# Hybrid encoder block on one Trainium2 core: short convolutions as closures among the next group's steps, side-stream loads issued a pause ahead

## Chip, cores and metric

The kernel runs on one core of a Trainium2 chip. The metric is the device time of one launch in microseconds (us). Three runs of the kernel before took 2955.26 to 2956.12 us, median 2955.6.

## What is computed

One block of a hybrid encoder on 512 tokens of width 2048, in fp32. Cut to what this case touches (the merge gates, the output projection and the feed-forward part come after it and stay as they are):

```python
hn = rmsnorm(x, norm1_w[l])
proj = hn @ w_in[l]
conv_out = centred_depthwise_conv(proj[..., :SHORT_CONV_CH], conv_w[l], conv_b[l])   # 3 taps
hv, hx1, hx2 = split of conv_out[..., :3 * HW]            # hyena: 3 x 1024 columns
z = hx1 * long_conv(hv, kf[:, 0], hb[0])                  # FFT convolutions with learned filters
y_a = hx2 * long_conv(z, kf[:, 1], hb[1])
q, k = silu(conv_out[..., 3 * HW:])                       # mLSTM: 4 heads of 256
v, o, g = rest of proj                                    # values, output gate, 16 gate columns
h_fwd, h_bwd = mlstm_direction(q, k, v, g), and on the reversed sequence
y_b = sigmoid(o) * (h_fwd + h_bwd)
merge = rest[..., 2 * MW + N_MLSTM_GATES:]
x = x + (sigmoid(merge_a) * (y_a @ w_branch_a) + sigmoid(merge_b) * (y_b @ w_branch_b)) @ w_out
x = x + (silu(gate) * up) @ w_down                        # after a second rmsnorm
```

## The kernel before

Every fp32 product is made of three matrix products of halves (`mm3`, L70): an operand is split into a high half `h` (a rounding copy on ScalarE, ACT) and a low half `l` (operand minus high half, on VectorE, DVE). For the weights these are `wh` (L164) and `wl` (L165).

The first stage multiplies the normalised input by the columns of `w_in` for hyena, heads and output gate. It goes by column groups of 256: twelve for hyena (four quarters `q`, three kinds each), then per head one for q, one for k and one for v, and four for the output gate, in the order of `parts`. A group has 8 steps of two 128-row blocks of weights; a step ends with `yield`. Weights are loaded by SyncE (SP, L157) and split two units ahead of use (`Weights`, `AHEAD`).

When a hyena, q or k group ends, `conv_evac` takes its two PSUM tiles. For each it multiplies by the row scale out of PSUM into a padded tile `pp` (L332), makes the middle tap with the bias on ACT (L334), adds the first tap (L336) and the last (L339 for hyena, where the result is written in four residue classes, L342 for q and k, with a SiLU on ACT behind it), all on DVE. Then a store on GpSimd's queue (POOL) takes the result to DRAM: `d_hy` (L356), `d_q` and `d_k` (L366). A v group is copied out of PSUM by ACT and stored to `d_v` (L374).

Between the steps of the main stream, `drive` (L242) advances a side stream. Each main step gives it a credit of `RATIO` = 2.2 (at most twice that is kept), and each piece of side work that yields a number costs that number. The side stream takes turns between two generators. One makes the hyena filters (`filter_net`, then `spectra`) and, last, combinations of the input for the next stage (`combos_x`). The other makes the gates, `hyena(q)` for each quarter and `mlstm(h)` for each head as soon as their columns have been stored. A generator that yields `"pause"` is left alone until two main steps later.

`hyena(q)` loads four tiles of `d_hy` by POOL (L750), transposes them on TensorE (PE, L683) into split halves (L314, L315) and makes the convolutions. `mlstm(h)` loads q and k by SP (L804), splits them at once, makes the scores `S`, loads `d_v` (L823) and the gate rows (L837) by POOL, and stores its result `d_yb` by POOL (L893).

The next stage (`Winograd`, loads `r` and `wr` at L1006 by SP, splits at L997 and L998) begins when main and side stream are through. `combo_1` prepares parts of its operands from the last output-gate group on, in tiles of the same pool as the side stream's (`gt`); three of its calls come after the main stream.

Of the kernel before, what the change touches and what calls it, by code (L numbers as in the profile page):

```python
# [11 lines left out]
ALU = mybir.AluOpType  # L12
# [22 lines left out]
def hybrid_block_kernel(ctx, tc, x, norm1_w, w_in, conv_w, conv_b, filt_w1, filt_b1, filt_freq1,  # L35
# [187 lines left out]
    def group_v(w, c0, act, ahead=None):  # L223

        ps = [mm_ps() for _ in range(4)]
        units = w_units(w, 0, KB, c0)
        for u in range(0, KB, 2):
            h, l = next(units) if ahead is None else ahead.get(c0, u)
            for tb in range(4):
                ts = slice(tb * P, (tb + 1) * P)  # L230
                for k in range(2):
                    kb = u + k
                    aH, aL = act[kb]
                    mm3(ps[tb][:, 0:256], aH[:, ts], aL[:, ts], h[:, k, :], l[:, k, :],
                        kb == 0, kb == KB - 1)
            yield None
        yield ps

    tick = [0]
    PAUSE = 2  # L240

    def drive(main, side=None, rate=0):  # L242

        left = 0
        for _ in main:
            tick[0] += 1
            left = min(left + rate, 2 * rate)
            while side is not None and left > 0:
                r = next(side, "wait")
                if r == "wait":  # L250
                    break
                left -= r
# [71 lines left out]
        return t.rearrange("p (m c) -> p c m", c=4)  # L324


    def conv_evac(ps, blk, classed):
        n_tile[0] += 1
        pp = pr.tile([P, L + 2], F32, tag="pp", name=f"pp_{n_tile[0]}", bufs=2)
        nc.gpsimd.memset(pp[:, 0:1], 0.0)  # L330
        nc.gpsimd.memset(pp[:, L + 1:L + 2], 0.0)
        nc.vector.tensor_tensor(pp[:, 1:L + 1], ps, rbc, ALU.mult)  # L332
        y = st()
        nc.scalar.activation(y, pp[:, 1:L + 1], AF.Identity, bias=cb[:, blk:blk + 1],  # L334
                             scale=cw[:, 1, blk:blk + 1])
        nc.vector.scalar_tensor_tensor(y, pp[:, 0:L], cw[:, 0, blk:blk + 1], y, ALU.mult, ALU.add)  # L336
        y2 = st()
        if classed:
            nc.vector.scalar_tensor_tensor(classes(y2), natural(pp[:, 2:L + 2]), cw[:, 2, blk:blk + 1],  # L339
                                           natural(y), ALU.mult, ALU.add)  # L340
        else:
            nc.vector.scalar_tensor_tensor(y2, pp[:, 2:L + 2], cw[:, 2, blk:blk + 1], y, ALU.mult, ALU.add)  # L342
            nc.scalar.activation(y2, y2, AF.Silu)
        return y2

    def hyena_cols(q, after_first=()):
        for kind in range(3):
            if kind == 1:
                yield from after_first
            for r in first_group if q == 0 and kind == 0 else group_feat(  # L350
                    w_in, 0, KB, kind * HW + q * 256, X, ahead=ahead):
                if r is None:
                    yield
            for j in range(2):
                y = conv_evac(r[j], kind * 8 + 2 * q + j, True)
                nc.gpsimd.dma_start(d_hy[kind][2 * q + j], y)  # L356
        done.add(("hy", q))

    def head_cols(h):
        for base, blk0, dst in ((C_Q, 24, d_q), (C_K, 32, d_k)):  # L360
            for r in group_feat(w_in, 0, KB, base + h * 256, X, ahead=ahead):
                if r is None:
                    yield
            for j in range(2):
                y = conv_evac(r[j], blk0 + 2 * h + j, False)
                nc.gpsimd.dma_start(dst[2 * h + j], y)  # L366
        done.add(("qk", h))
# [139 lines left out]
    h2 = {}  # L507

    def filter_net():
        for m in range(4):  # L510
            t = gt()
            nc.gpsimd.dma_start(t, c_dft[m])
            hh = new(ph, f"dH{m}", dt=F32R)
            ll = new(ph, f"dL{m}", dt=F32R)
            nc.scalar.copy(hh, t)
            nc.vector.tensor_tensor(ll, t, hh.bitcast(F32), ALU.subtract)
            dft.append((hh, ll))
            yield 1
# [10 lines left out]
        nc.gpsimd.dma_start(zt[0:33], c_zt)  # L529

        def sin_layer(ps, b, fr):
# [83 lines left out]
    def spectrum(q, o):  # L615
# [11 lines left out]
            wt.append(t)  # L627
        row = gt()
        nc.sync.dma_start(row[0:1, 0:256], hyena_bias[0][o:o + 1, c0:c0 + 256])
        yield .1  # L630
        wpm = gt()
        nc.vector.tensor_tensor(wpm[:, 0:256], w3[:, 0:256], w3[:, 256:512], ALU.add)
        nc.vector.tensor_tensor(wpm[:, 256:512], w3[:, 0:256], w3[:, 256:512], ALU.subtract)
# [109 lines left out]
    def hyena(q):  # L743
# [9 lines left out]

        u = load(0)
        x1 = load(1)
        yield .1
        halves = []
        for ps in by_times(u):
            halves.append(gsplit(ps))
# [37 lines left out]
    def mlstm(h):  # L797
        yield from need("gates")
        yield from need(("qk", h))
        qs, ks = [], []  # L800
        for src, dst in ((d_q, qs), (d_k, ks)):
            for j in range(2):
                t = gt()
                nc.sync.dma_start(t, src[2 * h + j])  # L804
                dst.append(gsplit(t))
            yield .6
        yield "pause"
        S = []
        for sb in range(4):
# [7 lines left out]
            yield .3  # L817
        yield from need(("v", h))

        V = []  # L820
        for b in range(2):
            t = gt()
            nc.gpsimd.dma_start(t.rearrange("p (b c) -> p b c", b=2),  # L823
                                d_v[h][2 * b:2 * b + 2].rearrange("b p c -> p b c"))
            vh, vl = vt(), vt()
# [7 lines left out]
        yield .6  # L833

        def load_row(d):
            t = gt()
            nc.gpsimd.dma_start(t, d_rows[4 * d + h:4 * d + h + 1].to_broadcast([P, L]))  # L837
            return t

        def weights(d, sb, row):  # L840

# [13 lines left out]


        units = [(0, sb) for sb in (0, 1, 2, 3)] + [(1, sb) for sb in (3, 2, 1, 0)]
        row = load_row(0)
        yield "pause"
        acc_t = [gt(), gt()]  # L860
        nxt = weights(*units[0], row)
        row_b = load_row(1)
# [124 lines left out]
    class Winograd:  # L987
# [30 lines left out]
        def cols(self, c0, psf, loaded=None, after={}, late=None):  # L1018
# [52 lines left out]
            nc.vector.tensor_tensor(C[1][:, hi], p5, u2, ALU.add)  # L1071
            return C

    N_PLAIN = 4
    AHEAD = 2
    RATIO = 2.2
    side = turns(stream_b(), stream_a())

    parts = (("hy", 1), ("hd", 0), ("hy", 2), ("hy", 3), ("hd", 1), ("hd", 2), ("hd", 3))
# [5 lines left out]
    def w_in_cols():  # L1085
# [9 lines left out]
    drive(w_in_cols(), side, RATIO)  # L1095
    for i in range(5, 8):
        combo_1(i, gt)
    for _ in side:
        tick[0] += 1
    pr_cm.__exit__(None, None, None)  # L1100
# [386 lines left out]
```

## Time and profile before

| | us |
|---|---|
| median of 3 runs | 2955.6 |
| the profiled execution, its own time | 2956.98 |
| its span | 2955.0 |
| PE busy in the span | 2893.7 |
| DVE busy | 2112.5 |
| ACT busy | 1271.5 |
| POOL busy | 185.7 |
| PE busy between 50 and 890 us | 805.29 of 840 |

The span is the time from the first to the last instruction on the core. An engine's busy time counts its compute instructions; issuing a transfer isn't counted. A wait is listed with the instruction that waited and, behind an arrow, the one that released it. The rows name tiles without their numbers: `sd` and `mm` are PSUM tiles, `g` tiles of the side stream's pool, `st` and `pp` those of the short convolution. The granted clock is the share of full speed that the chip gave PE; 1.00 is 2.4 GHz, 0.50 is 1.2 GHz.

### The profile page before, as it was taken

The page shows a single profiled execution, that of the slowest core. Times are in us where ns is not written, and L with a number is a line of the kernel's source. Part 1 is how long each engine was busy: PE and PEld are TensorE (multiplying, and loading weights), DVE is VectorE, ACT ScalarE, POOL GpSimd, SP SyncE. Part 2 cuts the span into 40 slices and gives each one's busy share as a digit, 9 for nine tenths or more (in the row PEclk, how much of TensorE's full clock was granted, in tenths as well). Part 3 has the DMA queues.
Part 4 walks back from the last instruction along what each step waited for, and adds up shares of the span by engine and source line. Part 5 has one row for each costly group of instructions (what it writes and reads, how often), then busy time and mean ns, then how long its engine had stood idle before and what let it go on. Part 6 is the DMA issues. An engine that isn't in the chain of part 4 may idle for free.

```text
span 2955.0 us, 48209 instructions
## 1 busy us (share of the span) xinstructions
PE 2893.7 (98%) x18412; PEld 2614.7 (88%) x18412; DVE 2112.5 (71%) x3843; ACT 1271.5 (43%) x2258; POOL 185.7 (6%) x433
## 2 busy tenths in 40 slices
PE   8999999998989999999999999999999999999998
PEld 6788887887879999888899999999999998888886
DVE  6897868777659888645448888888888886233336
ACT  5334344334555454422445444444444444233224
POOL 1011011101110000100010000000000000000000
PEclk9999999999999999999999999999999999999999
DMA  5333343333344444843444333333333336334333
GB/s 175 108 118 115 114 125 125 107 100 122 124 139 134 131 126 129 271 132 104 136 125 136 121 116 115 121 123 115 119 118 115 120 103 213 101 115 128 121 114 128
DMA packets 285185, 377.01 MB, mean 128 GB/s; under 512 B 18013, under 2 KB 221147, under 8 KB 284953
## 3 DMA queue, kind: packets, MB, share of 16 engines
q1 hardware_dynamic: 261280, 301.19, 32.9%
q0 software_dynamic: 22272, 70.55, 7.0%
q8 instruction: 144, 2.36, 0.3%
q10 hardware_dynamic: 1401, 2.20, 0.2%
q14 instruction: 88, 0.72, 0.1%
HBM read 326.67 MB, written 47.20 MB: 127 GB/s over the span
## 4 chain that ended last, share of the span: by engine, by line
PE 89%; DVE 4%; DMA 3%; issue 2%; ACT 1%; POOL 0%; SPq 0%; ACTq 0%; DVEq 0%; POOLq 0%
PE mm L70 63%; PE sd L70 25%; DMA wr<-in_w_down_dram 1%; DMA g<-d_hy 1%; DVE wl L165 0%; DMA hl<-d_h 0%; PE sd L683 0%; DMA g<-d_k 0%; DVE st L339 0%; DMA xt<-in_x_dram 0%; DVE st L336 0%; DVE h L81 0%; PE sd L1246 0%; DVE s L1014 0%; DMA g<-d_q 0%
## 5 line engine op out<-in xcount | busy, mean ns | idle before, releaser
L165 DVE TENSOR_TENSOR wl<-wr,wh 128x512 fp32r<-128x512 f32 x512 | 350.3, 689 | 492.9 <-ACT wh L164 485.8
L164 ACT CAST wh<-wr 128x512 fp32r<-128x512 f32 x512 | 315.8, 620 | 763.9 <-PE mm L70 722.1
L70 PE MATMUL mm<-a,wh 128*128 128x512 f32 (+1 forms) x2136 | 626.5, 377 | 0.0
L70 PE MATMUL mm<-T,h 128*128 128x256 f32 x2592 | 471.1, 284 | 3.2 <-ACT h L997 3.2
L70 PE MATMUL sd<-T,h 128*128 128x256 f32 x2592 | 468.2, 283 | 0.0
L70 PEld LDWEIGHTS mm<-a,wh 128*128 128x128 f32 x2136 | 388.8, 190 | 69.8 <-issue 2.9
L70 PEld LDWEIGHTS mm<-T,h 128*128 128x128 f32 x2592 | 406.3, 193 | 3.7 <-ACT h L997 3.7
L70 PE MATMUL mm<-a,wl 128*128 128x512 f32 (+1 forms) x1068 | 400.3, 376 | 8.2 <-DVE wl L165 6.1
L70 PEld LDWEIGHTS sd<-T,h 128*128 128x128 f32 x2592 | 404.4, 192 | 0.0
L70 PE MATMUL mm<-wh,h 128*128 128x512 f32 x1280 | 394.8, 389 | 2.8 <-ACT h L80 2.5
L70 PE MATMUL mm<-T,l 128*128 128x256 f32 x1296 | 368.0, 284 | 0.5 <-DVE l L998 0.5
L997 ACT CAST h<-s 128x512 fp32r<-128x512 f32 x395 | 244.5, 620 | 286.3 <-PE sd L70 142.1
L70 PE MATMUL sd<-T,l 128*128 128x256 f32 x1296 | 366.9, 283 | 0.0
L70 PEld LDWEIGHTS mm<-wh,h 128*128 128x128 f32 x1280 | 240.1, 188 | 54.0 <-ACT h L80 3.2
L998 DVE TENSOR_TENSOR l<-s,h 128x512 fp32r<-128x512 f32 x395 | 270.2, 685 | 11.6 <-ACT h L997 9.0
L997 ACT CAST h<-r 128x512 fp32r<-128x512 f32 x285 | 176.6, 620 | 222.6 <-PE mm L70 111.6
L70 PE MATMUL mm<-wh,a 128*128 128x256 f32 (+1 forms) x1152 | 262.5, 321 | 0.0
L70 PEld LDWEIGHTS mm<-T,l 128*128 128x128 f32 x1296 | 249.7, 193 | 1.0 <-DVE l L998 1.0
L70 PE MATMUL mm<-wl,h 128*128 128x512 f32 x640 | 249.0, 389 | 0.3 <-DVE wl L165 0.3
L70 PEld LDWEIGHTS sd<-T,l 128*128 128x128 f32 x1296 | 248.9, 192 | 0.0
L70 PEld LDWEIGHTS mm<-a,wl 128*128 128x128 f32 x1068 | 202.4, 190 | 46.8 <-DVE wl L165 9.2
L998 DVE TENSOR_TENSOR l<-r,h 128x512 fp32r<-128x512 f32 x285 | 191.6, 686 | 48.0 <-ACT h L997 47.6
(369 smaller groups left out, 4367.6 us busy)
## 6 DMA issues: line engine op xcount, KB each, us to landing
r<-in_w_gate_up_dram SPq DMA_DIRECT2D x176, 512.0 KB, 3.9
wr<-in_w_in_dram SPq DMA_DIRECT2D x144, 512.0 KB, 3.8
wr<-in_w_down_dram SPq DMA_DIRECT2D x88, 512.0 KB, 3.8
r<-in_w_in_dram SPq DMA_DIRECT2D x32, 512.0 KB, 4.5
wr<-in_w_out_dram SPq DMA_DIRECT2D x32, 512.0 KB, 3.7
d_h<-xo POOLq DMA_DIRECT2D x44, 256.0 KB, 2.6
hl<-d_h SPq DMA_DIRECT2D x44, 256.0 KB, 3.4
d_g<-xo POOLq DMA_DIRECT2D x32, 256.0 KB, 4.3
```

The costliest lines, as they stand in the source:

```text
L70: nc.tensor.matmul(o, a, b, start=start, stop=stop)
L164: nc.scalar.copy(h, src)
L165: nc.vector.tensor_tensor(l, src, h.bitcast(F32), ALU.subtract)
L997: nc.scalar.copy(h, a)
L998: nc.vector.tensor_tensor(l, a, h.bitcast(F32), ALU.subtract)
```

## The change

`conv_evac` does only the two multiplications out of PSUM at the group's end. The rest of each convolution, with its store, becomes a closure in the list `later`. `drive` pops one closure at each following main step, ahead of the side stream, and takes 1.9 from the side stream's credit for it. The marks that let `hyena` and `mlstm` begin (`done`) are closures too, at no cost, behind the stores.

`RATIO` goes from 2.2 to 2.6. Loads of the side stream are issued together, with a pause before their first use: in `filter_net`, `spectrum`, `hyena` and `mlstm`. The q and k loads of `mlstm` go to POOL's queue in place of SP's. `group_v` starts with two of the four token blocks and makes up for the other two in its second step. `combo_1` uses the `pp` tiles instead of the pool `g`.

```diff
@@ group_v
+            for tb, v, (wh, wl) in ([(tb, u, (h, l)) for tb in (0, 1)] + ([(2, 0, first), (3, 0, first)] if u == 2 else [])
+                                    + ([(2, u, (h, l)), (3, u, (h, l))] if u else [])):
...
@@ drive
             left = min(left + rate, 2 * rate)
+            if later:
+                cost, work = later.pop(0)
+                work()
+                left -= cost
             while side is not None and left > 0:
@@ conv_evac
         nc.vector.tensor_tensor(pp[:, 1:L + 1], ps, rbc, ALU.mult)
-        y = st()
...
+        def rest():
+            y = st()
+            nc.scalar.activation(y, pp[:, 1:L + 1], AF.Identity, bias=cb[:, blk:blk + 1],
+                                 scale=cw[:, 1, blk:blk + 1])
+            nc.vector.scalar_tensor_tensor(y, pp[:, 0:L], cw[:, 0, blk:blk + 1], y, ALU.mult, ALU.add)
...
+            store(y2)
+
+        later.append((1.9, rest))
+
+    def store_to(dst):
+        return lambda t: nc.gpsimd.dma_start(dst, t)
@@ hyena_cols
-                y = conv_evac(r[j], kind * 8 + 2 * q + j, True)
-                nc.gpsimd.dma_start(d_hy[kind][2 * q + j], y)
-        done.add(("hy", q))
+                conv_evac(r[j], kind * 8 + 2 * q + j, True, store_to(d_hy[kind][2 * q + j]))
+        later.append((0, lambda: done.add(("hy", q))))
@@ hyena
         x1 = load(1)
-        yield .1
+        yield "pause"
@@ mlstm
-        for src, dst in ((d_q, qs), (d_k, ks)):
+        raw = []
+        for src in (d_q, d_k):
             for j in range(2):
                 t = gt()
-                nc.sync.dma_start(t, src[2 * h + j])
-                dst.append(gsplit(t))
-            yield .6
+                nc.gpsimd.dma_start(t, src[2 * h + j])
+                raw.append(t)
+        yield "pause"
+        for dst in (qs, ks):
+            for j in range(2):
+                dst.append(gsplit(raw.pop(0)))
+                yield .7
...
@@ before the end of the stage
+    def padded():
+        n_tile[0] += 1
+        return pr.tile([P, L + 2], F32, tag="pp", name=f"pp_{n_tile[0]}", bufs=2)[:, 0:L]
...
-    RATIO = 2.2
+    RATIO = 2.6
...
-                    combo_1(n - 3, gt)
+                    combo_1(n - 3, padded)
```

The change moves instructions on most engines of the first stage; from the first products of the next stage on, the order is as before. Three places follow.

DVE where the q group of head 2 ends. Before, with the convolution's L336 (first tap) and L342 (last tap) of both tiles, among pieces of a hyena convolution (L709 to L718), up to the next `wl`:

```order
L336 SCALAR_TENSOR_TENSOR st_6223<-pp_6219,cols_86,st_6223 128x512
L709 TENSOR_TENSOR g_6214<-g_6185,g_5315 128x512
L342 SCALAR_TENSOR_TENSOR st_6226<-pp_6219,cols_86,st_6223 128x512
L710 TENSOR_TENSOR g_6185<-g_6186,g_5314 128x512
L336 SCALAR_TENSOR_TENSOR st_6234<-pp_6230,cols_86,st_6234 128x512
L711 TENSOR_TENSOR g_6214<-g_6214,g_6185 128x512
L342 SCALAR_TENSOR_TENSOR st_6237<-pp_6230,cols_86,st_6234 128x512
L714 TENSOR_TENSOR g_6215<-g_6213 128x256
L715 TENSOR_TENSOR g_6215<-g_6214 128x256
L717 TENSOR_TENSOR g_6185<-g_6213 128x256
L718 TENSOR_TENSOR g_6185<-g_6214 128x256
L165 TENSOR_TENSOR wl_6269<-wr_6243,wh_6268 128x512
```

Twenty-eight DVE instructions stand there between one `wl` and the next. The same convolution on DVE in the change (L344 is the multiplication out of PSUM, L350 and L356 the taps):

```order
L165 TENSOR_TENSOR wl_6176<-wr_6173,wh_6175 128x512
L344 TENSOR_TENSOR pp_6163<-mm_5831,rbc_534 128x512
L344 TENSOR_TENSOR pp_6167<-mm_5832,rbc_534 128x512
L350 SCALAR_TENSOR_TENSOR st_6191<-pp_6163,cols_86,st_6191 128x512
L165 TENSOR_TENSOR wl_6199<-wr_6173,wh_6198 128x512
L356 SCALAR_TENSOR_TENSOR st_6194<-pp_6163,cols_86,st_6191 128x512
L350 SCALAR_TENSOR_TENSOR st_6214<-pp_6167,cols_86,st_6214 128x512
L165 TENSOR_TENSOR wl_6268<-wr_6265,wh_6267 128x512
L356 SCALAR_TENSOR_TENSOR st_6217<-pp_6167,cols_86,st_6214 128x512
L165 TENSOR_TENSOR wl_6296<-wr_6265,wh_6295 128x512
```

At most three DVE instructions stand between two `wl` now.

POOL at the loads of hyena 2, before (L750 loads `d_hy`, L893 stores `d_yb` of head 0, L356 stores `d_hy`, L330 and L331 clear the ends of `pp`):

```order
L356 DMA d_hy_6_105<-st_4710 128x512
L330 MEMSET pp_4943 128x1
L331 MEMSET pp_4943 128x1
L750 DMA g_4647<-d_hy_4_95 128x512
L893 DMA d_yb_151<-g_4618 128x512
L893 DMA d_yb_152<-g_4626 128x512
L750 DMA g_4649<-d_hy_5_96 128x512
L750 DMA g_4651<-d_hy_4_103 128x512
L750 DMA g_4653<-d_hy_5_104 128x512
L356 DMA d_hy_7_106<-st_4720 128x512
```

and POOL at the same loads in the change (L770, L921, L363, L342 and L343; L877 belongs to head 0):

```order
L363 DMA d_hy_6_105<-st_4702 128x512
L877 AFFINE_SELECT g_4590<-g_4590 128x128
L342 MEMSET pp_4930 128x1
L343 MEMSET pp_4930 128x1
L363 DMA d_hy_7_106<-st_4724 128x512
L342 MEMSET pp_4934 128x1
L343 MEMSET pp_4934 128x1
L770 DMA g_4663<-d_hy_4_95 128x512
L921 DMA d_yb_151<-g_4652 128x512
L921 DMA d_yb_152<-g_4660 128x512
L770 DMA g_4665<-d_hy_5_96 128x512
L770 DMA g_4667<-d_hy_4_103 128x512
```

The store of `d_hy_7_106` has moved ahead of the loads; the two stores of head 0 stand between the first load and the others, as before.

The q and k loads of head 1. Before, on SP, among the weight loads (L157):

```order
L804 DMA g_7063<-d_q_117 128x512
L157 DMA wr_7357<-in_w_in_dram 128x4x256
L804 DMA g_7069<-d_q_118 128x512
L804 DMA g_7079<-d_k_125 128x512
L157 DMA wr_7436<-in_w_in_dram 128x4x256
L804 DMA g_7085<-d_k_126 128x512
```

and in the change on POOL (L363 are stores of head 3's q and k, L813 hyena 3's result):

```order
L363 DMA d_q_122<-st_7055 128x512
L825 DMA g_7079<-d_q_117 128x512
L813 DMA d_ya_149<-g_7064 128x512
L813 DMA d_ya_150<-g_7072 128x512
L825 DMA g_7081<-d_q_118 128x512
L825 DMA g_7083<-d_k_125 128x512
L825 DMA g_7085<-d_k_126 128x512
L363 DMA d_k_129<-st_7301 128x512
```

The four loads now stand on one queue with the stores of the convolutions and of hyena 3. For heads 2 and 3 the two stores of the head before stand at the place of `d_ya` here.

## Rows read from the trace of the kernel before

**Rows 1.** The page, busy us (share of the span) and instructions of each engine
```profile
PE 2893.7 (98%) x18412; PEld 2614.7 (88%) x18412; DVE 2112.5 (71%) x3843; ACT 1271.5 (43%) x2258; POOL 185.7 (6%) x433
```

**Rows 2.** Windows, 50 to 890 us: PE, PEld, DVE, ACT, POOL, PEclk, DMA, GB/s
```profile
50.00:890.00 840.00, 805.29 (x4289) 676.38 (x4289) 646.10 (x1282) 371.72 (x668) 97.59 (x262) 0.98 0.38 118
```

**Rows 3.** What PE waited for, 50 to 880 us: total us, times, longest
```profile
PE mm L70 <- DVE wl L165: 11.5, 6, 5.4
PE sd L683 <- DMA g<-d_hy: 10.3, 6, 4.5
PE sd L70 <- ACT g L314: 3.1, 2, 2.3
PE mm L70 <- DVE wl L998: 1.9, 1, 1.9
...
PE sd L70 <- DVE g L315: 1.1, 1, 1.1
```

**Rows 4.** Timeline of PE at stalls: start, us, instruction, [idle before, releaser]
```profile
457.30 0.88 PE L683 MATMUL sd<-csm,g 128*128 128x128 f32 x6 [1.07 <-DMA g<-d_hy]
...
583.76 0.44 PE L683 MATMUL sd<-csm,g 128*128 128x128 f32 x1 [4.50 <-DMA g<-d_hy]
...
616.48 0.50 PE L70 MATMUL mm<-a,wl 128*128 128x512 f32 x1 [1.84 <-DVE wl L165]
...
726.96 0.58 PE L70 MATMUL mm<-wl,a 128*128 128x256 f32 x1 [5.45 <-DVE wl L165]
...
883.53 0.79 PE L70 MATMUL mm<-a,h 128*128 128x256 f32 x2 [4.06 <-ACT h L997]
```

**Rows 5.** Timeline of DVE, 597 to 616 us
```profile
597.73 0.69 DVE L165 TENSOR_TENSOR wl<-wr,wh 128x512 fp32r<-128x512 f32 x1 [2.03 <-ACT wh L164]
600.45 0.69 DVE L165 TENSOR_TENSOR wl<-wr,wh 128x512 fp32r<-128x512 f32 x1 [2.03 <-ACT wh L164]
601.51 0.69 DVE L583 TENSOR_TENSOR g<-sd,g 128x512 f32<-128x512 f32 x1 [0.37 <-PE sd L70]
...
609.94 0.74 DVE L336 SCALAR_TENSOR_TENSOR st<-pp,cols,st 128x512 f32<-128x512 f32 x1
610.60 0.68 DVE L709 TENSOR_TENSOR g<-g,g 128x512 f32<-128x512 f32 x1
...
615.74 0.68 DVE L165 TENSOR_TENSOR wl<-wr,wh 128x512 fp32r<-128x512 f32 x1
```

**Rows 6.** Groups of POOL by line, 50 to 900 us: busy us, mean ns, idle before
```profile
L356 POOL DMA_DIRECT2D d_hy<-st x24 | 13.3, 555 | 244.5 <-DVE st L339 160.6 <-ACT wh L164 46.8 <-ACT g L592 28.5
L750 POOL DMA_DIRECT2D g<-d_hy x24 | 12.9, 541 | 13.8 <-PE sd L70 8.3 <-DVE g L647 4.9 <-issue 0.6
...
L893 POOL DMA_DIRECT2D d_yb<-g x8 | 4.3, 544 | 22.6 <-ACT g L892 22.6
```

**Rows 7.** DMA issues, 50 to 900 us: KB each, median us to landing
```profile
g<-d_hy POOLq DMA_DIRECT2D x24, 256.0 KB, 5.1
...
g<-d_q SPq DMA_DIRECT2D x8, 256.0 KB, 4.2
...
d_yb<-g POOLq DMA_DIRECT2D x8, 256.0 KB, 3.1
```

**Rows 8.** Timeline of SP's queue, 870 to 886 us
```profile
878.70 2.57 SPq L1006 DMA_DIRECT2D r<-in_w_in_dram  x4
```

**Rows 9.** Timeline of PE at the next stage's first products
```profile
878.95 0.40 PE L70 MATMUL mm<-a,wh 128*128 128x256 f32 x2
879.19 0.28 PE L70 MATMUL mm<-a,wl 128*128 128x256 f32 x1
```

**Rows 10.** Windows of PE behind three stalls: PE busy, PEclk, DMA share, GB/s
```profile
586.00:592.00 6.00, 6.00 (x24) 0.65 0.00 0
...
616.00:626.00 10.00, 9.52 (x35) 0.83 0.48 137
...
727.00:733.00 6.00, 5.84 (x34) 0.74 0.60 183
```

More of the change, by code (lines that the diff above doesn't have):

```diff
@@ L226, in group_v @@
         units = w_units(w, 0, KB, c0)
+        first = None
         for u in range(0, KB, 2):
             h, l = next(units) if ahead is None else ahead.get(c0, u)
-            for tb in range(4):
+            if u == 0:
+                first = (h, l)
+            for tb, v, (wh, wl) in ([(tb, u, (h, l)) for tb in (0, 1)] + ([(2, 0, first), (3, 0, first)] if u == 2 else [])
+                                    + ([(2, u, (h, l)), (3, u, (h, l))] if u else [])):
                 ts = slice(tb * P, (tb + 1) * P)
                 for k in range(2):
-                    kb = u + k
+                    kb = v + k
                     aH, aL = act[kb]
-                    mm3(ps[tb][:, 0:256], aH[:, ts], aL[:, ts], h[:, k, :], l[:, k, :],
+                    mm3(ps[tb][:, 0:256], aH[:, ts], aL[:, ts], wh[:, k, :], wl[:, k, :],
                         kb == 0, kb == KB - 1)
@@ L239, in hybrid_block_kernel @@
     tick = [0]
+    later = []
     PAUSE = 2
@@ L324, in natural, with conv_evac @@
         return t.rearrange("p (m c) -> p c m", c=4)
-    def conv_evac(ps, blk, classed):
+    def conv_evac(ps, blk, classed, store):
         n_tile[0] += 1
@@ L332, in conv_evac @@
         nc.vector.tensor_tensor(pp[:, 1:L + 1], ps, rbc, ALU.mult)
-        y = st()
[L334 to L344, printed above, removed]
+        def rest():
[3 more added lines that the diff above has]
+            nc.vector.scalar_tensor_tensor(y, pp[:, 0:L], cw[:, 0, blk:blk + 1], y, ALU.mult, ALU.add)
+            y2 = st()
+            if classed:
+                nc.vector.scalar_tensor_tensor(classes(y2), natural(pp[:, 2:L + 2]), cw[:, 2, blk:blk + 1],
+                                               natural(y), ALU.mult, ALU.add)
+            else:
+                nc.vector.scalar_tensor_tensor(y2, pp[:, 2:L + 2], cw[:, 2, blk:blk + 1], y, ALU.mult, ALU.add)
+                nc.scalar.activation(y2, y2, AF.Silu)
+            store(y2)
+        later.append((1.9, rest))
+    def store_to(dst):
+        return lambda t: nc.gpsimd.dma_start(dst, t)
     def hyena_cols(q, after_first=()):
@@ L364, in head_cols @@
             for j in range(2):
-                y = conv_evac(r[j], blk0 + 2 * h + j, False)
-                nc.gpsimd.dma_start(dst[2 * h + j], y)
-        done.add(("qk", h))
+                conv_evac(r[j], blk0 + 2 * h + j, False, store_to(dst[2 * h + j]))
+        later.append((0, lambda: done.add(("qk", h))))
         for r in group_v(w_in, C_V + h * 256, X, ahead):
@@ L509, in filter_net @@
     def filter_net():
+        tables = []
         for m in range(4):
@@ L512, in filter_net @@
             nc.gpsimd.dma_start(t, c_dft[m])
[L513 to L518, printed above, removed]
+            tables.append(t)
         vec = new(ph, "fvec", (P, 4))
@@ L529, in filter_net @@
         nc.gpsimd.dma_start(zt[0:33], c_zt)
+        yield "pause"
+        for m, t in enumerate(tables):
+            hh = new(ph, f"dH{m}", dt=F32R)
+            ll = new(ph, f"dL{m}", dt=F32R)
+            nc.scalar.copy(hh, t)
+            nc.vector.tensor_tensor(ll, t, hh.bitcast(F32), ALU.subtract)
+            dft.append((hh, ll))
+            yield 1
         def sin_layer(ps, b, fr):
@@ L755, in hyena @@
         x1 = load(1)
-        yield .1
+        yield "pause"
         halves = []
@@ L800, in mlstm @@
         qs, ks = [], []
-        for src, dst in ((d_q, qs), (d_k, ks)):
+        raw = []
+        for src in (d_q, d_k):
             for j in range(2):
                 t = gt()
-                nc.sync.dma_start(t, src[2 * h + j])
-                dst.append(gsplit(t))
-            yield .6
+                nc.gpsimd.dma_start(t, src[2 * h + j])
+                raw.append(t)
+        yield "pause"
+        for dst in (qs, ks):
+            for j in range(2):
+                dst.append(gsplit(raw.pop(0)))
+                yield .7
         yield "pause"
@@ L818, in mlstm, with load_row @@
         yield from need(("v", h))
+        def load_row(d):
+            t = gt()
+            nc.gpsimd.dma_start(t, d_rows[4 * d + h:4 * d + h + 1].to_broadcast([P, L]))
+            return t
         V = []
+        raw = []
         for b in range(2):
@@ L824, in mlstm @@
                                 d_v[h][2 * b:2 * b + 2].rearrange("b p c -> p b c"))
+            raw.append(t)
+        row = load_row(0)
+        yield "pause"
+        for t in raw:
             vh, vl = vt(), vt()
@@ L832, in mlstm @@
                 V.append((vh[:, k, :], vl[:, k, :]))
[L833 to L838, printed above, removed]
+            yield .7
         def weights(d, sb, row):
@@ L857, in mlstm @@
         units = [(0, sb) for sb in (0, 1, 2, 3)] + [(1, sb) for sb in (3, 2, 1, 0)]
-        row = load_row(0)
-        yield "pause"
         acc_t = [gt(), gt()]
@@ L1091, in w_in_cols @@
                 if g == 3 and 3 <= n < 8:
-                    combo_1(n - 3, gt)
+                    combo_1(n - 3, padded)
                 yield
     drive(w_in_cols(), side, RATIO)
+    assert not later
     for i in range(5, 8):
-        combo_1(i, gt)
+        combo_1(i, padded)
     for _ in side:
```

## Prediction

> **What bounds the kernel now.** I read the page first. TensorE (PE) is busy for 98% of the span [rows 1], so whatever the change gains must come out of PE's few idle stretches. The diff touches the first stage only, which ends near 880 us. Between 50 and 890 us PE is busy for 805.29 of 840 us [rows 2], so 34.7 us of idle time is to be had, plus what PE loses where its clock is lower: the mean granted clock of that stretch is 0.98.
>
> The next view is the list of what PE waited for [rows 3]. Four kinds matter: `wl`, the low half of the split weights that VectorE (DVE) makes (11.5 us in 6 waits); the loads of `d_hy` for the hyena transposes (10.3 in 6); the splits of the q and k loads (3.1 and 1.1); and one wait on L998 as the next stage begins (1.9). With the 4.06 us wait for a weight tile `r`, which falls behind the list's window [rows 4], they make 32.0 of the 34.7 us.
>
> The third view is PE's timeline at the longest stalls [rows 4], and the fourth what DVE did then. For the 1.84 us stall at 616.48 it shows [rows 5] that no `wl` is made between 600.45 and 615.74, and that DVE goes from one operation to the next from 601.51 on. Earlier it made a `wl` every 2.72 us (that is one step of a column group) and idled 2.03 us before it. So DVE isn't short of time on average. It is late where the work at a group's end piles up with that of the side stream.
>
> **The change part by part.**
> *Closures.* At a group's end only the two multiplications out of PSUM stay. The other four convolution operations (first and last tap, twice) go into the next group's first two steps, one pair each. In the 615.74 stretch each takes 0.66 us (starts at 609.94 and 610.60), 2.64 us together. Taken out from ahead of the `wl` they cover the 1.84 us stall. In the new order a `wl` stands among them after every second one, as the fences on DVE show. The longest stall, 5.45 us at 726.96, is not covered by 2.64 alone. But there the old order has 43 DVE instructions between two `wl`, six of them a convolution's. In the new order the longest such stretch behind the stage's start has 28, with none of a convolution, because each closure costs the side stream 1.9 of its credit in the step it shares. I count 10 us of the 11.5 as gone, and leave 1.5 for one place where a `wl` still stands close to its use. Bounds: 0 (DVE's total is the same) and 11.5.
>
> *Pauses on the hyena loads.* Two ticks are two steps, 5.4 us more between issue and first transpose. The longest wait that this must cover is 4.50 us, of hyena 3 [rows 4]; it and those of hyena 0 and 1 are covered, 9.2 us. Not so hyena 2's, 1.07 us at 457.30. There the store of its own group's last convolution and two stores of the head before now stand ahead of or among the four loads on POOL, as the fences on POOL show. An issue takes 0.54 us, and stores wait for their data, 10 us in the mean on L356 [rows 6], so the two steps are used up. I leave the 1.1 us. Bounds 4 and 10.3.
>
> *q and k loads.* They leave SP for POOL: 16 issues of 0.54 us, 8.7 us on a queue that is busy for 97.59 of 840 us [rows 2, 6]. The pause gives them 5.4 us. POOL's `d_hy` loads land in 5.1 us where SP's q and k loads take 4.2 [rows 7], and POOL's in-order waits come on top. Two waits are head 1's and covered. The third, 2.3 us, is head 3's [rows 3]; there the loads stand behind stores of head 2 that wait for copies on ScalarE, and I leave 1.5. Gain 2.7 of 4.2, bounds −4 (two heads 2 us worse each) and 4.2.
> The `d_v` and filter loads get the same pause; no wait in the list is for them, so nothing.
>
> *The V group's order, one more table load on ScalarE.* The new order of the token blocks takes the K group's banks one step later, by when DVE has freed them. No wait of the list is for that: nothing. I take off 0.6 us for one wait on ScalarE, whose copies of V now follow closer (an estimate: one copy's 0.62 us). A table load is hidden, with ScalarE busy 43% [rows 1].
>
> *The stage's end.* `combo_1` now works on the convolution's `pp` tiles, and its chain no longer holds back L998: 1.9 us go. The four `r` loads were issued at 878.70 [rows 8], and PE could go on at 883.53, 4.83 us later. Now the first of the late two waits for the last head's transposes (their end be T), the second for the landing of that head's last store: copy 0.62, issue 0.54 and landing 3.1 us [rows 7], so at T+4.3. With 4.83 behind each issue PE gets them at T+4.9 and T+9.1. Counting the products in the new order at 0.12 us each (0.40 us for two, 0.28 for one [rows 9]) it reaches them at T+3.9 and, with the first us lost, T+6.4. Lost are 3.7 us in place of 6.0 (1.9 and 4.06): gain 2.3, bounds −3 and 5.
>
> *The clock.* Behind the three longest stalls of the middle PE's clock drops from its 2.4 GHz level to 1.2 for a few us: the mean grant is 0.65 over 586 to 592, 0.83 over 616 to 626, 0.74 over 727 to 733 [rows 10]. That is 2.1, 1.7 and 1.6 us lost, which go with the stalls: 5.4, bounds 0 and 7 (two shorter drops more).
>
> **The sum.** 10 + 9.2 + 2.7 + 2.3 + 5.4 − 0.6 = 29.0 us. The profiled execution took 2956.98 us (span 2955.0); that gives 2928.0. It lies 1.4 us above the median of the runs shown, 2955.6, so the median should come to 2926.6, rounded **2927**.
>
> **The rivals.** About 0.2% (6 us) is what a measurement of this kernel can tell from no change.
>
> *A. DVE stays late.* The work is moved, not removed, and DVE is busy for 646.10 of the 840 us [rows 2]. If the piles only shift, the 11.5 us stay, and so do the clock's losses behind two of them (3.3): the gain is 29 − 10 − 3.3 = 15.7, the time 2940. For it: the side stream's credit per step goes up from 2.2 to 2.6. Against it: the 2.03 us idle before a `wl` in an ordinary step [rows 5].
>
> *B. The loads move behind the new queue.* POOL runs in order, and its loads stand among stores that wait for DVE and ScalarE. If hyena 2 and 3 and heads 2 and 3 each wait 3 us (between the 4.50 and 2.3 of before), the loads' 12 us are given back: 2939.
>
> *C. Slower: stores block q and k.* The place is the row of POOL's order where a head's loads follow stores. L356's 24 stores waited 244.5 us, 10.2 each [rows 6]. If the loads of the three later heads and of hyena 2 each stood behind such a wait with the pause used up, 41 us would be lost. Against the 29 gained that is 12 more than now: 2968. It decides once a store's data come more than the pause's 5.4 us late. Against it: the stores next to those loads are rather L893's, which waited 22.6 us in 8 [rows 6].
>
> *D. DVE holds up POOL's issues.* If a load issued by POOL comes late whenever DVE is busy, the q and k loads lose what separates POOL's landing from SP's, 0.9 us each and four in a chain: 3.6 us a head, 10.8 for the three later heads, 2938. What the trace says against it: the 24 `d_hy` loads took 541 ns each to issue, though DVE was busy three quarters of the time. The Trainium skill, "SBUF — State Buffer", warns of just this in its box on the "DVE blocks DMA" trap: descriptors of a DMA issued from GpSimd are written by GpSimd, which is locked out while VectorE runs an operation in a two-port mode; it advises the SP or ACT queue. The page gives about 620 ns alone and 3100 ns overlapped; by that, an estimate, 16 loads would come some 40 us later in all and the kernel would be slower. The trace's uniform issue times do not agree with it for these operations.
>
> **How the numbers follow.** The forecast gets 0.73, A 0.09, B 0.09, C 0.04, D 0.05. With all upper bounds at once the median would be 2918, with all lower ones 2959. They are separate causes, so I take the forecast's own range as 2915 (all bounds and some smaller idle time that the list doesn't name) to 2936 (a third of the gain missing). A, B and D lie at 2938 to 2940. The range 2915 to 2943 takes them in with 3 us for a bad term, and leaves out C and the tails. Faster by over 0.2% are the forecast and most of A, B and D (0.90), within 0.2% the worst mixtures of them (0.06), slower is C (0.04).
>
> **What would show it.** In the changed profile: PE's waits for `wl` down to some 2 us; for `d_hy` to about 1, at hyena 2 alone; 1 to 2 for the last head's splits; two short stalls on `r` near 850 us, where the next stage would now begin; the granted clock at 1.00 where it was 0.65 to 0.83. It would be wrong if waits for `wl` stood at other groups' ends with the same sum (A), if PE waited for `d_hy`, `d_q` or `d_k` behind POOL rows that idle for a store (B, C), or if POOL's issues took over 1 us (D).

## The result, and the profile after

The changed kernel takes 2924.1 us (median of 4 runs, 2923.35 to 2925.4) against 2955.9 us of the kernel before on the same chip: ratio 0.9891, 95% interval [0.9874, 0.9908]. The forecast was 2927 in a range from 2915 to 2943. The gain is 31.7 us where 29 were summed up.

The page of the changed kernel, busy us of each engine and its share of the span:

```profile
span 2921.3 us, 48184 instructions
...
PE 2883.2 (99%) x18412; PEld 2611.4 (89%) x18412; DVE 2112.2 (72%) x3843; ACT 1272.4 (44%) x2259; POOL 195.5 (7%) x449
```

Against [rows 1] two things come apart. PE's idle time (span less busy time) went from 2955.0 − 2893.7 = 61.3 us to 2921.3 − 2883.2 = 38.1, so 23.2 us less. And the same 18412 matmuls were busy for 10.5 us less, most of it by the clock (worked out below). DVE's busy time is the same to 0.3 us. No arithmetic was saved; it came at better times. POOL's busy time grew by 9.8 us with 16 more instructions, the issues of the q and k loads (0.54 us each): other than stated ahead of the prediction, what POOL spends on issuing a transfer is counted on the page.

The windows view of the stage, to 860 us now (columns as in [rows 2]), and the list of what PE waited for, up to 880 us (total us, times, longest):

```profile
50.00:860.00 810.00, 799.85 (x4337) 676.84 (x4336) 650.43 (x1291) 375.13 (x676) 107.06 (x278) 1.00 0.40 124
```

```profile
PE mm L70 <- ACT h L1025: 3.8, 1, 3.8
PE sd L70 <- ACT g L324: 1.3, 1, 1.3
PE sd L703 <- DMA g<-d_hy: 1.1, 1, 1.1
PE mm L70 <- DVE wl L165: 1.0, 1, 1.0
...
PE sd L70 <- DVE g L325: 0.5, 1, 0.5
PE mm L70 <- DVE wl L1026: 0.5, 1, 0.5
...
PE mm L70 <- ACT wh L1025: 0.4, 1, 0.4
```

This answers to [rows 3]. The waits for `wl` fell from 11.5 us in 6 to 1.0 in one, those for `d_hy` from 10.3 in 6 to 1.1 in one, those of the q and k splits from 3.1 and 1.1 to 1.3 (the 0.5 at L325 is a split of a hyena convolution, not of q or k). The mean clock of the stage is 1.00 where it was 0.98. What is left is the start of the next stage. PE's timeline there, and SP's queue and ScalarE's timeline beside it:

```profile
845.20 0.50 PE L70 MATMUL mm<-a,h 128*128 128x256 f32 x2 [3.79 <-ACT h L1025]
...
848.41 0.79 PE L70 MATMUL mm<-a,wh 128*128 128x256 f32 x2 [0.35 <-ACT wh L1025]
...
849.69 0.58 PE L70 MATMUL mm<-a,wl 128*128 128x256 f32 x1 [0.49 <-DVE wl L1026]
```

```profile
837.77 7.68 SPq L1034 DMA_DIRECT2D r<-in_w_in_dram  x4
```

```profile
844.53 0.62 ACT L1025 CAST h<-r 128x512 fp32r<-128x512 f32 x1 [4.29 <-DMA d_o<-st]
847.74 0.62 ACT L1025 CAST wh<-r 128x512 fp32r<-128x512 f32 x1 [2.60 <-DMA r<-in_w_in_dram]
```

The two stalls that the prediction named are there, the first one larger and the second smaller. The bracket of the first split names a release that the prediction did not see: the store of the last output-gate group (`d_o`), whose tile `st` the split's tile `h` has to wait for, most likely as the two lie at the same place.

The new order of DVE shows in its timeline where the q group of head 2 ends, the place of [rows 5]:

```profile
580.19 0.69 DVE L344 TENSOR_TENSOR pp<-mm,rbc 128x512 f32<-128x512 f32 x1 [0.19 <-PE mm L70]
...
582.82 0.68 DVE L165 TENSOR_TENSOR wl<-wr,wh 128x512 fp32r<-128x512 f32 x1
583.42 0.74 DVE L356 SCALAR_TENSOR_TENSOR st<-pp,cols,st 128x512 f32<-128x512 f32 x1
584.08 0.74 DVE L350 SCALAR_TENSOR_TENSOR st<-pp,cols,st 128x512 f32<-128x512 f32 x1
584.75 0.69 DVE L165 TENSOR_TENSOR wl<-wr,wh 128x512 fp32r<-128x512 f32 x1
```

No operation of the side stream stands among them any more.

### The profile page after: what moved, and what is told of

It is laid out like the page before. It is cut to its first block, busy times and chain, and to the rows that moved or that the text cites. A ratio compares the mean times of both kernels' runs of the same rounds, so it can differ in the third digit from the quotient of the medians.

```text
span 2921.3 us, 48184 instructions
## 1 busy us (share of the span) xinstructions
PE 2883.2 (99%) x18412; PEld 2611.4 (89%) x18412; DVE 2112.2 (72%) x3843; ACT 1272.4 (44%) x2259; POOL 195.5 (7%) x449
## 4 chain that ended last, share of the span: by engine, by line
PE 93%; DVE 3%; DMA 2%; issue 1%; ACT 1%; POOL 0%; SPq 0%; ACTq 0%; DVEq 0%; POOLq 0%
PE mm L70 67%; PE sd L70 26%; DMA wr<-in_w_down_dram 1%; DVE wl L165 0%; DMA xt<-in_x_dram 0%; DVE st L353 0%; PE sd L703 0%; PE sd L1279 0%; PE sd L280 0%; DVE h L81 0%; DMA g<-d_q 0%; DMA d_yb<-g 0%; DMA g<-d_hy 0%; DVE st L350 0%; DVE T L1307 0%
## 5 line engine op out<-in xcount | busy, mean ns | idle before, releaser
L1025 ACT CAST h<-s 128x512 fp32r<-128x512 f32 x395 | 244.8, 621 | 285.4 <-PE sd L70 141.9
L1026 DVE TENSOR_TENSOR l<-s,h 128x512 fp32r<-128x512 f32 x395 | 270.6, 686 | 12.1 <-ACT h L1025 9.7
L1025 ACT CAST h<-r 128x512 fp32r<-128x512 f32 x285 | 176.8, 620 | 221.4 <-PE mm L70 111.2
L1026 DVE TENSOR_TENSOR l<-r,h 128x512 fp32r<-128x512 f32 x285 | 192.1, 688 | 51.9 <-ACT h L1025 51.6
```

The lines of the kernel that those rows point to most:

```text
L1025: nc.scalar.copy(h, a)
L1026: nc.vector.tensor_tensor(l, a, h.bitcast(F32), ALU.subtract)
```

## The experiments

The runs of an experiment are compared with runs of the kernel before made beside them (medians 2954.1 to 2956.4 us). Times of different experiments that lie within some 6 us (0.2%) of each other are not told apart by the runs; there the waits in the traces have to decide.

The first two experiments take the change's first part apart. The closures do two things: they move the rest of a convolution into the next group's steps, and they charge 1.9 for it to the side stream. Theory M says that the moving relieves DVE, theory R that the charge does.

**The charge without the moving.**

```diff
-        later.append((1.9, rest))
+        rest()
+        later.append((1.9, lambda: None))
```

> The changed kernel with the rest of each convolution done at once at the group's end again, as before the change; the charge of 1.9 per convolution on the side stream's credit stays, and so do all pauses. Theory M (moving the four convolution operations behind the next weights is what relieves DVE): PE's waits for wl come back, some 10 us and 3 us of clock, so about 2937 us. Theory R (the charge is what relieves it: beside a group's end the side stream issues less, so that DVE's work does not pile up): waits for wl stay at 1 to 3 us in all, 2924 to 2927 us. The order of DVE, where few wl stand close to their use in this kernel, speaks for R.

Measured: 2925.6 us (2925.05 to 2926.39), ratio 0.9901 [0.9887, 0.9916]. PE's waits for `wl` in its list:

```profile
PE mm L70 <- DVE wl L165: 1.7, 1, 1.7
```

Of the two, R holds, and the reason can be seen in DVE's timeline at the end of the same q group:

```profile
583.75 0.69 DVE L344 TENSOR_TENSOR pp<-mm,rbc 128x512 f32<-128x512 f32 x1 [0.20 <-PE mm L70]
...
586.38 0.68 DVE L165 TENSOR_TENSOR wl<-wr,wh 128x512 fp32r<-128x512 f32 x1
586.98 0.74 DVE L356 SCALAR_TENSOR_TENSOR st<-pp,cols,st 128x512 f32<-128x512 f32 x1
587.64 0.74 DVE L350 SCALAR_TENSOR_TENSOR st<-pp,cols,st 128x512 f32<-128x512 f32 x1
588.30 0.69 DVE L165 TENSOR_TENSOR wl<-wr,wh 128x512 fp32r<-128x512 f32 x1
```

It is the order of the changed kernel. The code issues the whole convolution at once, and yet `wl` of later steps stand among its operations: the step that builds the program sorts each engine's instructions. Of the 1328 DVE instructions of the first stage in this trace, 1295 stand in the same order as in the changed kernel's trace (lined up by operation, tile names and shape), against 455 in the kernel before, and 708 in the next experiment, which has the closures but not the charge. With the charge in place, the closure as such moves next to nothing. What is left to it of the time, 1.5 us, is less than the runs can tell; 1.3 us of it stand at the next stage's start, where PE waits 5.1 us in place of 3.8.

**The moving without the charge.**

```diff
-        later.append((1.9, rest))
+        later.append((0, rest))
```

> The changed kernel with closures that cost the side stream nothing (0 in place of 1.9), so that its credit of 2.6 a step is paid in full. Theory M: wl waits stay near 1 us and the side stream ends some 60 us earlier, which takes away the stall on the r tiles (about 6 us): 2917 to 2920 us. Theory R: DVE's piles come back, wl waits of 8 to 15 us at the ends of hyena and q, k groups with 3 us or more of clock behind them, less the 6 us of the r stall: 2929 to 2938 us.

Measured: 2931.6 us (2928.77 to 2932.44), ratio 0.9918 [0.9902, 0.9935], in R's range of times. Seven waits for `wl` are back, in all less than the 8 to 15 us that R gave:

```profile
PE mm L70 <- DVE wl L165: 6.2, 7, 1.3
...
PE mm L70 <- ACT h L1025: 2.1, 1, 2.1
```

The side stream ends some 55 us earlier (its last transposes start at 783.1 us, in the change at 837.6), but the wait for the `r` tiles only fell from 3.8 to 2.1 us. The split that it waits for stands idle for 2.73 us until the store of `d_o` has landed, here too.

**The credit and the charge on the kernel before.** Two kernels, without closures and without pauses. The first raises the credit:

```diff
-    RATIO = 2.2
+    RATIO = 2.6
```

> The kernel before with RATIO 2.6 in place of 2.2 and nothing else changed. Theory R (DVE's piles come from how much side work is issued beside a group's end): more wl waits than before, 15 to 25 us of them in place of 11.5, with a lower clock behind them; the side stream ends some 60 us earlier, which gives back a few us at the r tiles; 2956 to 2966 us. If the credit hardly matters (theory M): 2950 to 2955 us, from the r tiles alone.

The second adds the charge:

```diff
     def conv_evac(ps, blk, classed):
+        later.append(1.9)
...
             left = min(left + rate, 2 * rate)
+            if later:
+                left -= later.pop(0)
...
-    RATIO = 2.2
+    RATIO = 2.6
```

> The kernel before with RATIO 2.6 and the charge of 1.9 per convolution, taken from the credit of the step behind it; convolutions run at once at the group's end, no pauses are added, q and k stay on SP. Theory R: the charge alone, without closures or pauses, takes away about half of the 11.5 us of wl waits and the clock behind them: 2943 to 2949 us, with the waits for d_hy (about 10 us) and for the q and k splits unchanged. Theory M: the wl waits stay or grow, 2953 to 2960 us.

Measured: 2982.6 us for the first (ratio 1.0095 [1.0079, 1.0112]) and 2952.8 for the second (0.9993 [0.9983, 1.0002]), against 2954.1 of the kernel before. The first is 28 us slower than the kernel before, and 17 us beyond the upper end of R's range. Its waits of PE:

```profile
PE mm L70 <- DVE wl L165: 26.7, 13, 5.1
```

The 26.7 us are just beyond the range that R gave. PE's busy time (2905.1 us on its page, 11.4 more than before) adds what the lower clock costs (mean grant of the execution 0.990, before 0.993). The second has the `wl` waits that R said, half of those of before, but misses R's range of times:

```profile
PE sd L687 <- DMA g<-d_hy: 8.4, 6, 3.2
PE mm L70 <- ACT h L1001: 6.5, 1, 6.5
PE mm L70 <- DVE wl L165: 5.6, 5, 2.6
PE sd L70 <- ACT g L317: 5.1, 5, 1.8
```

The `d_hy` loads stay late, the q and k splits are a little later (5.1 us), and at the end PE waits 6.5 us for the first `r` tile. So the charge repairs what the higher credit breaks, some 30 us, and the two together are worth nothing that can be measured against the kernel before.

The kernels with the credit of 2.6 can now be set side by side. PE's waits for `wl` are 26.7 us with neither charge nor pauses, 5.6 with the charge alone, 6.2 with the pauses (and the change's other parts) but no charge, 1.0 to 1.7 with both; the times are 2982.6, 2952.8, 2931.6 and 2924.1 to 2925.6 us. At this credit the pauses with the change's other parts are worth more (51 us) than the charge (30), and on top of them the charge is worth 6 to 8. A kernel with the pauses at this credit and neither closures nor charge was not run, so whether the moving helps where nothing is charged stays open.

**The pauses alone, on the kernel before.** The regrouped loads and pauses as in the change, q and k on POOL; no closures and no charge, RATIO 2.2, the old order in the V group, `combo_1` in the pool `g`. The regrouped code of `mlstm` also asks more credit for its splits of q, k and v, 4.2 a head (six times 0.7) in place of 1.8.

```diff
...
-        later.append((1.9, rest))
+        rest()
...
-    RATIO = 2.6
+    RATIO = 2.2
...
-                    combo_1(n - 3, padded)
+                    combo_1(n - 3, gt)
```

> The kernel before with the pauses and the regrouped loads alone (q and k on POOL too): convolutions at once at the group's end, no charge, RATIO 2.2, the old order of the V group, combo_1 in the pool g. If pauses only cover loads: the d_hy waits fall from 10 to 1 to 3 us, wl waits stay near 11 us, and the side stream, which the pauses make late, ends some 8 us of TensorE work behind the main stream, which costs 8 to 15 us at the end: 2945 to 2955 us. If pauses also spread DVE's work: wl waits of 3 to 6 us, 2938 to 2948 us.

Measured: 2944.6 us (2944.3 to 2945.9), ratio 0.9964 [0.9951, 0.9977]; in the second range of times.

```profile
PE sd L70 <- ACT g L877: 9.1, 6, 3.1
...
PE mm L70 <- DVE wl L165: 2.9, 2, 1.8
...
PE sd L698 <- DMA g<-d_hy: 1.3, 2, 1.0
```

The `wl` waits fell from 11.5 to 2.9 us without closures or charge. Covering loads can't be all that the pauses do. That the arithmetic behind a load comes two steps later, and falls less often on a group's end, is the likely reason; it was not shown apart from the higher credit that the splits cost. The other side of it is the first row, with waits in the last head's chain (L877). The side stream is late and has no main stream left to hide behind. The windows of the stage's end show it (columns as in [rows 2]):

```profile
840.00:860.00 20.00, 10.84 (x52) 9.21 (x51) 12.24 (x35) 11.55 (x29) 3.30 (x8) 0.66 0.04 14
860.00:880.00 20.00, 13.30 (x72) 11.68 (x73) 11.98 (x24) 6.59 (x14) 1.10 (x2) 0.66 0.40 132
```

**The changed kernel with the old credit.**

```diff
-    RATIO = 2.6
+    RATIO = 2.2
```

> The changed kernel with RATIO 2.2 in place of 2.6. The charge takes 3.8 of 17.6 credits per convolution group, so the side stream falls behind: in the order its last transposes come some 38 us of TensorE work behind the main stream's end, in a chain of small steps that nothing covers. 15 to 50 us slower than the changed kernel: 2940 to 2975 us, with wl waits at 1 us or less. If the side stream's rate did not matter: 2924 us.

In this kernel `combo_1` rewrites halves of the input before the late `combos_x` has read them, so that the combinations for the next stage are made from other numbers; the amount of work is the same. Measured: 2991.5 us (2 runs), ratio 1.0122 [1.0101, 1.0142], slower than expected.

```profile
PE sd L70 <- ACT g L882: 25.9, 16, 6.0
PE sd L70 <- ACT g L324: 13.8, 2, 7.2
```

```profile
800.00:850.00 50.00, 30.25 (x131) 25.69 (x132) 27.00 (x71) 24.02 (x59) 9.57 (x24) 0.67 0.19 64
850.00:900.00 50.00, 31.37 (x128) 26.78 (x126) 21.29 (x57) 21.50 (x54) 9.47 (x26) 0.68 0.16 53
```

There is no `wl` wait in its list at all, and yet it is 67 us slower than the change: the side stream's rest runs bare for some 110 us (the main stream's last wide products end at 795 us, the side stream's last transposes start at 906). The credit has to be high enough to finish in time, and the charge and the pauses make that credit bearable.

**Without the pause of the hyena loads.**

```diff
         x1 = load(1)
-        yield "pause"
+        yield .1
```

> The changed kernel without the pause behind the d_hy loads of hyena (0.1 of credit as before the change); all else stays. If the pause is what covers these loads: PE waits for d_hy again, 8 to 11 us in all, with 2 to 3 us of clock, about 2935 us. If the loads are early enough anyway since the side stream's turn comes later: 2 to 3 us of waits, 2926 us. The d_q and d_k waits should stay as they are.

Measured: 2928.7 us (2927.07 to 2930.89), ratio 0.9912 [0.9897, 0.9927], between the two expectations.

```profile
PE sd L703 <- DMA g<-d_hy: 5.0, 5, 1.5
PE mm L70 <- DVE wl L165: 3.3, 4, 1.2
```

This pause takes 3.9 us from the `d_hy` waits and 2.3 from those for `wl`. The other half of the 9.2 us on `d_hy` goes without it; that the rationed side stream and the other pauses place these loads better is the likely reason, and was not taken apart.

**The q and k loads on SP, with the pause kept.**

```diff
-                nc.gpsimd.dma_start(t, src[2 * h + j])
+                nc.sync.dma_start(t, src[2 * h + j])
```

> The changed kernel with the q and k loads of mlstm on SP's queue again, with the pause kept. Theory D (VectorE holds up what POOL issues): loads land earlier on SP, the 1.3 us wait before the last head's scores goes, 2921 to 2923 us. My reading (the queue hardly matters, the pause does): 2923 to 2926 us, with landings within 1 us of those on POOL; SP's loads can come later where a weight load that waits for its buffer stands ahead of them.

Measured: 2923.0 us (2921.64 to 2923.32), ratio 0.9892 [0.9877, 0.9906]: the queue is worth nothing that can be measured. The time lies where the two expectations meet, so the traces have to tell them apart. In the changed kernel, with the loads on POOL, the view of the loading line gives the issue times (ns, least, median, most):

```profile
L825 POOL DMA_DIRECT2D g<-d_q x8: 544/544/562, 374.4 to 791.6; - x8
L825 POOL DMA_DIRECT2D g<-d_k x8: 539/542/544, 390.4 to 792.7; - x8
```

The loads of the changed kernel land in 3.6 and 4.8 us (d_q, d_k) from POOL; in this experiment SP's take 4.0 and 5.1. Theory D has them land sooner on SP, and they don't. The wait before the last head's scores is gone on SP all the same. POOL's queue in the changed kernel shows why: three of the four loads stand behind head 2's stores, which wait for a copy on ScalarE.

```profile
786.04 0.56 POOL L825 DMA_DIRECT2D g<-d_q  x1 [0.22 <-POOL g L877]
790.33 0.54 POOL L921 DMA_DIRECT2D d_yb<-g  x1 [3.73 <-ACT g L920]
...
791.63 0.54 POOL L825 DMA_DIRECT2D g<-d_q  x1
```

SP issues the same loads from 786.85 to 788.6 us. So what POOL's queue costs there is its order, 1.3 us, and not VectorE. The `r` stall is 5.7 us on SP in place of 3.8, and the two about cancel.

**The V group's old order, and `combo_1` in the old pool.** Two kernels, each with one part of the change undone: `group_v` as before, and

```diff
-                    combo_1(n - 3, padded)
+                    combo_1(n - 3, gt)
...
-        combo_1(i, padded)
+        combo_1(i, gt)
```

> The changed kernel with the old order of the token blocks in the V group. My sum says this part is worth nothing: 2924 us within 1.5 us, no wait of PE for DVE's L344. If it is worth something, PE waits for L344 at the three or four V groups, 0.5 to 2 us each: 2926 to 2931 us.

> The changed kernel with combo_1 in tiles of the side stream's pool again (gt in place of padded). My sum says 2 us come back at L1026 (1.9 before) and the r loads wait for combo_1 as before, 4 us in one stall: 2925 to 2928 us. If the pp tiles changed nothing: 2924 us.

Measured: 2925.6 us for the first (2922.93 to 2926.14; 0.9897 [0.988, 0.9913]), with no wait of PE for L344: nothing that can be told, as summed. 2927.4 for the second (2925.82 to 2928.91; 0.9908 [0.9893, 0.9923]), which the interval does not tell from the change either. Its stall at L1025 is 6.1 us where the change has 3.8, and no wait of 1.9 us at L1026 came back, so the 2 us are right by the trace and their place is not.

**The stage's end.** The side stream gets 3.4 a step during the output-gate groups, so that it ends before the main stream, and the last three `combo_1` work in a PSUM tile.

```diff
+            rate = tail_rate[0] or rate
             left = min(left + rate, 2 * rate)
...
+        tail_rate[0] = 3.4
         for g in range(4 - N_PLAIN, 4):
...
-        combo_1(i, padded)
+        combo_1_psum(i)
```

> The changed kernel with a credit of 3.4 a step (not 2.6) during the four output-gate groups, so that the side stream ends about 17 us of TensorE work before the main stream, and with the last three combo_1 in a PSUM tile, so that the r tiles wait for neither. If the stall on the r tiles (about 6 us with its clock) comes from the late end of the side stream, it goes: 2917 to 2920 us. If it is the landing itself, or DVE is late in the output-gate groups at the higher credit: 2923 to 2927 us.

Measured: 2922.9 us (2919.24 to 2923.91), ratio 0.9891 [0.9876, 0.9905]. SP's queue, ScalarE's timeline and PE's tell why it isn't more:

```profile
833.74 2.02 SPq L1048 DMA_DIRECT2D r<-in_w_in_dram  x4
```

```profile
846.97 0.62 ACT L1039 CAST h<-r 128x512 fp32r<-128x512 f32 x1 [2.73 <-DMA d_o<-st]
```

```profile
847.64 0.50 PE L70 MATMUL mm<-a,h 128*128 128x256 f32 x2 [1.98 <-ACT h L1039]
```

All four `r` loads are issued by 835.8, some 10 us before PE has nothing else to do (847.64 less 1.98 us), and the split still comes at 846.97: it waits for the store of the last output-gate group. That was the last release in the changed kernel too (4.29 us, `d_o<-st`), so this experiment moved something that did not come last. The stall is shorter, 2.0 us for 3.8, because the store got through sooner. POOL issues it, in the changed kernel and in this one:

```profile
840.24 0.54 POOL L402 DMA_DIRECT2D d_o<-st  x1 [0.56 <-ACT a L1009]
```

```profile
844.53 0.54 POOL L404 DMA_DIRECT2D d_o<-st  x1 [0.65 <-ACT st L403]
```

In both kernels PE runs out of other work 1.1 to 1.2 us behind this issue. The split starts 4.29 us behind it in the change and 2.44 here. In the change the `r` loads were issued around the same time (837.77 to 845.45); that they held up the store is likely, and was not taken apart.

The last kernel puts that group's results into another pool:

```diff
         for j in range(2):
-            y = st()
+            y = gt() if g == 3 else st()
```

> As e8_tail, and the last output-gate group's results go into tiles of the pool g in place of st, so that the first split of an r tile does not wait for their store to land. If that store is what still holds PE there (2.0 us and its clock): the stall goes, 2919 to 2921 us. If not: 2922 to 2923 us, with the same 2 us at L1039.

Measured: 2918.9 us (2915.81 to 2920.66), ratio 0.9875 [0.986, 0.989], 5.2 us below the change, with every run below the change's fastest. The intervals of the two ratios overlap, so the time alone does not settle it; the trace does. The split follows the work before it without a wait, and PE's list has no wait for the first `r` tile:

```profile
844.86 0.60 ACT L1039 CAST h<-r 128x512 fp32r<-128x512 f32 x1
```

Over 840 to 860 us PE is busy for 19.0 of 20 us at a mean grant of 1.00; in the change these were 15.2 us at 0.83. This is the fastest kernel of the study. Whether moving the store alone, without the earlier end of the side stream, would have done as much was not run.

## Why the prediction was right, and which step was not

The time was right, 2924.1 for 2927. Taken by terms:

- *Waits for `wl`, 10 us of 11.5.* 10.5 went. The size is right partly by luck, since the step that gave the reason failed: "taken out from ahead of the `wl` they cover the 1.84 us stall". With the convolution issued at once at the group's end, and the charge kept, the kernel is as fast within 1.5 us and 1295 of the stage's 1328 DVE instructions keep their order. The order quoted ahead of the prediction was read as the effect of the closures, since the diff has them; it is the effect of the charge, which the prediction gave second place, and of the pauses, to which it gave no part in `wl`. On the kernel before, the pauses with their regrouped loads took 8.6 of the 11.5 us.
- *`d_hy`, 9.2 us.* 9.2 went, and hyena 2's wait of 1.1 us stayed where it was expected. The pause on these loads accounts for less than half of it directly.
- *q and k, 2.7 us.* 2.9 went: 1.3 us remain of 3.1 and 1.1, at the last head as expected.
- *V group, 0 and −0.6.* Nothing measurable.
- *The end, 2.3 us.* Mis-sized. Of 6.0 us (1.9 and 4.06) 5.0 remained (3.8, 0.4, 0.5 and pieces), so 1.0 was gained. The step that failed is the first of the two `r` tiles at "T+4.9": it left out the last output-gate store as a release. With the last head's transposes ending at 837.84 (T), PE reached the first tile at T+3.6, close to the T+3.9 of the prediction, and got it at T+7.4.
- *The clock, 5.4 us.* Mis-sized, the largest error of the sum: PE's busy time fell by 10.5 us, beyond the upper bound of 7. The three drops of [rows 10] were not all, and the window of the first began too late. The windows of the kernel before (columns as in [rows 2]):

```profile
270.00:280.00 10.00, 8.02 (x55) 7.82 (x54) 2.31 (x4) 2.92 (x6) 0.00 (x0) 0.83 0.29 102
372.00:382.00 10.00, 9.73 (x30) 6.14 (x29) 9.82 (x18) 4.22 (x8) 0.00 (x0) 0.83 0.19 58
583.00:590.00 7.00, 5.91 (x22) 5.06 (x23) 1.38 (x2) 2.35 (x4) 0.00 (x0) 0.52 0.22 86
```

  That is 1.7, 1.7 and 3.4 us (the prediction had 0, 0 and 2.1), with the other two some 10 us in all, an estimate from the mean grants. In the changed kernel the grant is 1.00 over 50 to 838 us. Behind the `r` stall it falls as it did before: 0.83 over 840 to 860 us, before 0.52 over 880 to 886.

Idle time was summed to 23.6 us (10 + 9.2 + 2.7 + 2.3 − 0.6) and measured as 23.2, by errors that cancel: 0.5 and 0.2 more on `wl` and on q and k, 0.6 not lost at the V groups, 1.3 less at the end. Between the two profiled executions 33.6 us went; the 4.6 beyond the sum are about what the clock term lacks.

Of the rivals, A (DVE stays late) did not come, but its argument that the higher credit piles up work was right and stronger than thought: it is the 28 us that RATIO 2.6 costs alone. B and C did not come: no load but hyena 2's and the last head's was late, and the last head's 1.3 us come from the order that B and C name. D did not come: POOL's issues of the q and k loads took 539 to 562 ns, and loads from SP do not land sooner.

The Trainium skill's box on the "DVE blocks DMA" trap in "SBUF — State Buffer" ties the trap to VectorE operations in a two-port mode. The same page says, in "Who interferes with whom", that `tensor_tensor` has no such mode, and 1085 of the 1310 DVE operations between 50 and 870 us are of that kind. The trace's uniform issue times are in line with that, and the prediction's estimate of 40 us applied the page's figure to operations for which it isn't meant.

## What to carry to other kernels

When a side stream fills the gaps of a main stream, count against its budget what the main stream itself puts on the shared engine at that moment. A higher budget without that cost 28 us here in the kernel without pauses and 6 to 8 us in the kernel with them; a lower one left the side stream's tail bare, 67 us. A pause that is meant to cover a load also moves the work behind the load: count that too. Where the program's builder sorts instructions, code written later isn't executed later: undo the textual part alone, and compare the built orders, before giving it the gain. A wait with several releases shows only the last one: take that one away first, and then look which stands next.

## What the runs showed of the hardware

Where a bare chain of small steps ran, the mean granted clock of PE was 0.66 to 0.68 over 20 to 50 us, a mixture of its levels 0.50 (1.2 GHz) and 1.00 (2.4 GHz), though it was busy for more than half of the time (30.25 of 50 us between 800 and 850 in the kernel with the old credit). An uncovered tail therefore costs its idle time and a second part in slower matmuls: the same 18412 matmuls were busy for 2904.8 us in that kernel and 2883.2 in the change.
